# Low parts of the wide merge-gate weights formed by accumulating transfers from GpSimd

## The chip, the core and the metric

The kernel runs on one core of one Trainium2 chip. The core has a matrix engine (TensorE, PE in the profile, with its weight loads as PEld), a vector engine (VectorE, DVE), an activation engine (ScalarE, ACT), a general engine (GpSimd, POOL), a queue that issues transfers (SyncE, SP), and 16 DMA engines that carry out the transfers of all queues. The metric is the device time of one execution in microseconds (us), the median of several runs.

## What is computed

One layer of a hybrid decoder block on 512 tokens of width 2048, in float32. The part that matters here is the large input projection and the merge at the end:

```
u    = rmsnorm(x)                      # 512 x 2048
proj = u @ w_in                        # w_in: 2048 x 20528
...                                    # mLSTM branch -> h_a, gated DeltaNet branch -> h_b
gate_a, gate_b = last 2 x 2048 columns of proj
y    = sigmoid(gate_a) * (h_a @ w_out[:2048]) + sigmoid(gate_b) * (h_b @ w_out[2048:])
out  = rmsnorm(x + y)
```

The columns of `proj` from 16432 on are the pre-activations of the merge gates: 4096 columns, two per output channel.

## The kernel before

**Products in two parts.** Matrix products are made of operands of type float32r, which carry fewer bits than float32. To keep accuracy each operand is split into a high part (the value rounded to float32r) and a low part (what rounding left). A product is the sum of three: high x high, high x low, low x high. For the activations u the two parts are made once (`uh`, `ul`). For the weights they are made on the fly from each raw tile.

**The weight stream.** A list `plan` holds every weight part in the order of use: 768 parts, each 256 KB. A part is either two row blocks of 128 rows by 256 columns (kind "i"), one row block by 512 columns of `w_in` (kind "w"), or the same of `w_out` (kind "o"). Three steps are taken for each part, and each runs ahead of the products:

- `load_raw` (line 135) takes a buffer of the ring `wr` (4 buffers) and lets SP issue the transfer from memory (line 145).
- `split_next` (line 148) takes a buffer each of the rings `wh` and `wl` (4 buffers each). ACT copies the raw tile into the float32r high part (`split_hi`, line 112). DVE subtracts that from the raw tile and writes the low part (`split_lo`, line 115).
- `next_w` (line 157) hands the parts to the products. When part i is used, raw loads up to part i + 4 and splits up to part i + 3 have been written down.

A buffer is reused as soon as its last reader is done: a raw buffer after the two split instructions, a `wh`/`wl` buffer after the last matmul of the part.

**The order of work.** PE's instructions run in the order in which the program writes them. On the other engines a scheduler places the instructions by priority; the loads and splits are raised above the rest. Each engine then runs its queue in order: an instruction that waits holds up all behind it.

**The stages.** First the activations and the projections of the two branches run as twelve units, with the work of the branches filled in between. Then come the merge gates (the loop of line 880): four narrow blocks of 256 columns (`proj_tm`, kind "i", lines 226 to 229), and six wide blocks of 512 columns (`proj_wide`, kind "w", lines 241 to 243). A wide block has 16 parts; a part is used by 12 matmuls, three for each of the four groups of 128 tokens, in the order uh x high, uh x low, ul x high. At the end of a block ACT makes the tanh of four PSUM tiles (line 895) and SP stores them to memory (line 896). Last comes the output projection (kind "o", lines 935 to 937).

While the wide blocks run, the branch output `h_a` is loaded back for the output projection: `load_h` (line 862) loads 16 tiles `hr` through the same ring `wr` (line 867) and splits them on ACT and DVE into `hh` and `hl` with the same two functions. `load_x` (line 872) loads x again into `hf`.

GpSimd issues no transfer anywhere in this kernel. Kind "w" also occurs earlier, for the values of the mLSTM branch (columns 2048 to 4095).

Of the kernel before, what the change touches and what calls it, by code (L numbers as in the profile page):

```python
# [8 lines left out]
F32 = mybir.dt.float32  # L9
F32R = mybir.dt.float32r  # L10
AF = mybir.ActivationFunctionType
ALU = mybir.AluOpType
# [3 lines left out]
P = 128  # L16
# [6 lines left out]
NO = 512  # L23
# [14 lines left out]
GATE = 16432  # L38
# [9 lines left out]
def hybrid_block(  # L48
# [18 lines left out]
    V, A, G, T = nc.vector, nc.scalar, nc.gpsimd, nc.tensor  # L67
# [43 lines left out]
    def split_hi(hi, src):  # L111
        A.copy(hi, src)  # L112

    def split_lo(lo, src, hi):
        V.tensor_tensor(out=lo, in0=src, in1=hi.bitcast(F32), op=ALU.subtract)  # L115


    plan = []
# [13 lines left out]
    raws, parts = [], []  # L132
# [15 lines left out]
    def split_next():  # L148
        raw, nk, n = raws[len(parts)]
        with tc.high_priority(offset=2 * PRIO if len(parts) > SAHEAD else 0):  # L150
            hi = wp.tile([P, nk, n], F32R, tag="wh", name="wh", bufs=NSPL)
            lo = wp.tile([P, nk, n], F32R, tag="wl", name="wl", bufs=NSPL)
            split_hi(hi, raw)
            split_lo(lo, raw, hi)
        parts.append((hi, lo))

    def next_w(kind, c, k):
        i = used[0]
        assert plan[i] == (kind, c, k)
        used[0] += 1  # L160
        while len(raws) < min(len(plan), i + RAHEAD + 1):
            load_raw()
        while len(parts) < min(len(plan), i + SAHEAD + 1):
            split_next()
        return parts[i]
# [755 lines left out]
    for nb in range(D // NO):  # L921
        nsl = slice(nb * NO, (nb + 1) * NO)
        for br in range(2):
# [19 lines left out]
            for kt in range(KT - last):  # L943
                w = next_w("o", nb * NO, base + kt)
# [52 lines left out]
```

## Time and profile before

| What | Value |
|---|---|
| Median of 3 runs | 2379.36 us (2378.52 to 2379.41) |
| The profiled execution | 2379.44 us |
| Its span in the trace | 2377.7 us, granted clock 0.998 |
| Transfers over the whole span | 265.94 MB, mean 112 GB/s |
| Casts of a weight part to its high part (line 112) | 768, 475.7 us, 621 ns each |
| Subtractions for its low part (line 115) | 768, 550.1 us, 718 ns each |
| Matmuls of the wide gate blocks | 1152, 389 ns each, pipelined |
| Loads of a raw part issued by SP | 768 of 256 KB, 2.8 us (w_in) and 3.1 us (w_out) to landing, median |

The span is the time from the first to the last recorded instruction of one execution; some 1.7 us of the execution lie around it. Busy times of matmuls overlap, since the next one starts before the last has drained: the length of one (389 ns) is not the pace at which they start. A row of the timeline gives the start, the length, the engine, the line, the operation, the tile written and the tiles read, and in brackets how long the engine stood idle before it and what ended that.

### The profile page before, as it was taken

The numbers are of one execution on the slowest core, as the hardware profiler recorded it, in microseconds if no ns is written. First come the engines' busy times: TensorE is split into PE (matmuls) and PEld (weight loads), VectorE is DVE, ScalarE is ACT, GpSimd is POOL, SyncE is SP. The second block draws the span as 40 slices with busy tenths as digits, with TensorE's granted clock in tenths as the row PEclk, the third lists the DMA queues.
The fourth block names the chain that finished last, engine by engine and source line by source line (L and its number), as shares of the span: only waits on it lengthen the run. The fifth ranks groups of instructions, "written<-read, shape, count | busy, mean of one in ns | idle before, by whom it ended". The sixth has DMA issues, their size and how long they took to land. (4 is left out here: it accounts for less than half of the span.)

```text
span 2377.7 us, 32465 instructions
## 1 busy us (share of the span) xinstructions
PE 2344.2 (99%) x11999; PEld 1953.4 (82%) x11999; DVE 1145.5 (48%) x2307; ACT 826.5 (35%) x1854; POOL 237.0 (10%) x319
## 2 busy tenths in 40 slices
PE   6999999999999999999999999999999999999998
PEld 5888888888888888888888888888998888888886
DVE  5433767433485833348583324958333222434334
ACT  5323434332343423243343224433333323322222
POOL 0000212100021210011220002112000000010010
PEclk9999999999999999999999999999999999999999
DMA  5433334333333333333342333333375544634333
GB/s 147 114 96 102 94 100 100 94 98 98 98 94 98 107 89 98 97 94 98 96 120 74 107 97 92 96 93 103 91 233 147 159 115 122 207 114 128 121 115 129
DMA packets 232354, 265.94 MB, mean 112 GB/s; under 512 B 46337, under 2 KB 171490, under 8 KB 232194
## 3 DMA queue, kind: packets, MB, share of 16 engines
q1 hardware_dynamic: 232130, 263.79, 39.1%
q8 instruction: 94, 1.54, 0.3%
q14 instruction: 66, 0.54, 0.1%
q10 hardware_dynamic: 64, 0.07, 0.0%
HBM read 239.61 MB, written 24.18 MB: 111 GB/s over the span
## 5 line engine op out<-in xcount | busy, mean ns | idle before, releaser
L115 DVE TENSOR_TENSOR wl<-wr,wh 128x512 fp32r<-128x512 f32 x768 | 550.1, 718 | 875.3 <-ACT wh L112 850.3
L112 ACT CAST wh<-wr 128x512 fp32r<-128x512 f32 x768 | 475.7, 621 | 1148.5 <-PE pj L212 565.4
L211 PE MATMUL pj<-uh,wh 128*128 128x512 f32 x1792 | 736.4, 411 | 2.1 <-ACT yp L442 1.6
L213 PE MATMUL pj<-uh,wl 128*128 128x512 f32 x1792 | 701.4, 391 | 0.0
L212 PE MATMUL pj<-ul,wh 128*128 128x512 f32 x1792 | 699.9, 391 | 0.0
L213 PEld LDWEIGHTS pj<-uh,wl 128*128 128x128 f32 x1792 | 336.5, 188 | 74.5 <-DVE wl L115 0.4
L211 PEld LDWEIGHTS pj<-uh,wh 128*128 128x128 f32 x1792 | 337.4, 188 | 67.1 <-ACT yp L442 2.9
L212 PEld LDWEIGHTS pj<-ul,wh 128*128 128x128 f32 x1792 | 337.9, 189 | 60.5
L935 PE MATMUL py<-wh,hh 128*128 128x512 f32 x512 | 199.2, 389 | 0.0
L936 PE MATMUL py<-wl,hh 128*128 128x512 f32 x512 | 199.2, 389 | 0.0
L937 PE MATMUL py<-wh,hl 128*128 128x512 f32 x512 | 199.2, 389 | 0.0
L241 PE MATMUL pg<-wh,uh 128*128 128x512 f32 x384 | 149.4, 389 | 0.0
L242 PE MATMUL pg<-wl,uh 128*128 128x512 f32 x384 | 149.4, 389 | 0.0
L243 PE MATMUL pg<-wh,ul 128*128 128x512 f32 x384 | 149.4, 389 | 0.0
L936 PEld LDWEIGHTS py<-wl,hh 128*128 128x128 f32 x512 | 96.1, 188 | 20.1
L935 PEld LDWEIGHTS py<-wh,hh 128*128 128x128 f32 x512 | 96.1, 188 | 20.0
L937 PEld LDWEIGHTS py<-wh,hl 128*128 128x128 f32 x512 | 96.1, 188 | 19.8
L241 PE MATMUL pv<-wh,uh 128*128 128x512 f32 x256 | 99.6, 389 | 0.0
L242 PE MATMUL pv<-wl,uh 128*128 128x512 f32 x256 | 99.6, 389 | 0.0
L243 PE MATMUL pv<-wh,ul 128*128 128x512 f32 x256 | 99.6, 389 | 0.0
L530 DVE TENSOR_TENSOR tmp<-ls,xi 32x31 f32<-32x31 f32 (+15 forms) x248 | 91.1, 367 | 5.2 <-DMA ls<-ld 1.7
L532 DVE TENSOR_TENSOR xi<-xi,tmp 32x31 f32<-32x31 f32 (+15 forms) x248 | 87.0, 351 | 4.0
(249 smaller groups left out, 2457.8 us busy)
## 6 DMA issues: line engine op xcount, KB each, us to landing
wr<-in_w_in_dram SPq DMA_DIRECT2D x640, 256.0 KB, 2.8
wr<-in_w_out_dram SPq DMA_DIRECT2D x128, 256.0 KB, 3.1
hr<-h_d SPq DMA_DIRECT2D x32, 256.0 KB, 3.5
tgl<-tg_d SPq DMA_DIRECT2D x32, 256.0 KB, 3.3
tg_d<-tgw SPq DMA_DIRECT2D x24, 256.0 KB, 3.8
xt<-in_x_dram SPq DMA_DIRECT2D x8, 512.0 KB, 9.0
gb<-rows_d SPq DMA_DIRECT2D x16, 256.0 KB, 3.4
h_d<-mg SPq DMA_DIRECT2D x16, 256.0 KB, 3.1
```

Of the source, the lines that this page charges most:

```text
L112: A.copy(hi, src)
L115: V.tensor_tensor(out=lo, in0=src, in1=hi.bitcast(F32), op=ALU.subtract)
L211: T.matmul(ps[j], hi[:, k, wsl], uh[:, kt, :], start=(kt == 0), stop=False)
L212: T.matmul(ps[j], hi[:, k, wsl], ul[:, kt, :], start=False, stop=False)
L213: T.matmul(ps[j], lo[:, k, wsl], uh[:, kt, :], start=False, stop=(kt == KT - 1))
L241: T.matmul(ps[c], uh[:, kt, tsl], hi[:, 0, :], start=(kt == 0), stop=False)
L242: T.matmul(ps[c], uh[:, kt, tsl], lo[:, 0, :], start=False, stop=False)
L243: T.matmul(ps[c], ul[:, kt, tsl], hi[:, 0, :], start=False, stop=(kt == KT - 1))
L530: V.tensor_tensor(out=tv, in0=ls[:, i, i + 1:BS].unsqueeze(2).to_broadcast([NSYS, n, m]), in1=xi[:, i, 0:m].unsqueeze(1).to_broadcast([NSY ...
L935: T.matmul(ps[c], hh[base][:, kt, tsl], hi[:, 0, :], start=(kt == 0), stop=False)
L936: T.matmul(ps[c], hh[base][:, kt, tsl], lo[:, 0, :], start=False, stop=False)
L937: T.matmul(ps[c], hl[base][:, kt, tsl], hi[:, 0, :], start=False, stop=(kt == KT - 1))
```

## The change

For the wide merge-gate blocks, 96 of the 768 parts, the subtraction on DVE is replaced by two steps. ACT writes minus the high part into the low tile. Then GpSimd issues a transfer that reads the same 128 x 512 piece of `w_in` from memory once more and adds it onto the low tile in SBUF, so that the tile ends as raw minus high. The raw load by SP and the cast by ACT stay; all other parts are split as before.

```diff
             hi = wp.tile([P, nk, n], F32R, tag="wh", name="wh", bufs=NSPL)
             lo = wp.tile([P, nk, n], F32R, tag="wl", name="wl", bufs=NSPL)
             split_hi(hi, raw)
-            split_lo(lo, raw, hi)
+            kind, c, k = plan[len(parts)]
+            if kind == "w" and c >= GATE:
+
+                A.mul(lo, hi.bitcast(F32), -1.0)
+                G.dma_start(lo[:, 0, :], w_in[k * P:(k + 1) * P, c:c + NO], accum_op=ALU.add)
+            else:
+                split_lo(lo, raw, hi)
         parts.append((hi, lo))
```

## The prediction

> **What bounds the kernel now.** I read the busy shares first, then the stretch that the change touches, then the order of work inside it.
>
> ```profile
> PE 2344.2 (99%) x11999; PEld 1953.4 (82%) x11999; DVE 1145.5 (48%) x2307; ACT 826.5 (35%) x1854; POOL 237.0 (10%) x319
> 1756.70:2017.80 261.10, 261.10 (x1154) 216.20 (x1153) 75.56 (x111) 81.30 (x134) 0.00 (x0) 1.00 0.48 139
> ACT wh L112 <- PE pg L243: 155.9, 81, 2.1
> ACT hh L112 <- DMA hr<-h_d: 19.3, 12, 5.4
> ACT tgw L895 <- DMA tg_d<-tgw: 1.9, 4, 0.7
> ```
>
> The first line is the page: PE is busy for 99% of the span. The second is the table by stretches, for the six wide merge-gate blocks (first matmul into pg at 1756.7, last at 2017.6 us): its columns are length, sum, PE, PEld, DVE, ACT, POOL (busy and count), granted clock, DMA share and GB/s. PE is busy for all 261.1 us at clock 1.00, DVE for 75.56, POOL for none; DMA moves 139 GB/s at a share of 0.48. The last three lines are from the waits of that stretch. PE is in none of them: the split waits for PE, never PE for the split. So nothing can be gained here; PE time can be lost, if a low part arrives late.
>
> How much room there is comes from the timeline inside a quiet block:
>
> ```profile
> 1868.42 0.62 ACT L112 CAST wh<-wr 128x512 fp32r<-128x512 f32 x1 [2.10 <-PE pg L243]
> 1871.14 0.62 ACT L112 CAST wh<-wr 128x512 fp32r<-128x512 f32 x1 [2.10 <-PE pg L243]
> 1870.94 0.39 PE L241 MATMUL pg<-wh,uh 128*128 128x512 f32 x1
> 1871.80 0.69 DVE L115 TENSOR_TENSOR wl<-wr,wh 128x512 fp32r<-128x512 f32 x1 [2.03 <-ACT wh L112]
> ```
>
> Columns: start, length, instruction, idle before and its releaser. Casts come every 2.72 us: one weight part is 12 matmuls, so PE's pitch is 0.227 us. A cast starts when PE has finished the part four earlier, 0.20 us after the next part's first matmul (1870.94). That cast is for the part that starts three parts later, whose second matmul is the first to read the low part: 1870.94 + 3 x 2.72 + 0.23 = 1879.33. Today the low part is there at 1872.49, 6.84 us early. That is the whole cover.
>
> **What the change does, step by step.**
>
> Removed: 96 subtractions on DVE (6 blocks x 16 parts), 96 x 0.692 = 66 us of DVE. DVE is 29% busy here and nothing waits for it except SP, which reloads a raw buffer after the subtraction. Worth 0 on the path; raw buffers come free one subtraction (0.69 us) earlier, and the cast finds its raw part already landed, so that is 0 too.
>
> Added on ACT: 96 negations of 128x512. The nearest row is ACT's own ACTIVATE of 128x512 from SBUF to SBUF (the tanh of line 448, 632 ns); taken 0.63 us. ACT's groups hold a single table load in the whole kernel, although scaled copies (lines 284, 823) already alternate with tanh, so no reload is counted. ACT goes from 81 to 142 us of 261: not a bound. Cast, handover 0.04 and negation put the transfer's start at 0.62 + 0.04 + 0.63 + 0.04 = 1.33 us after the cast's start. What is left for issue plus landing is 1879.33 - 1871.14 - 1.33 = 6.86 us.
>
> Added on POOL: 96 issues. POOL has nothing else between 1716 and about 2080 us, so nothing is queued behind them but the next issue. The trace has no transfer issued by POOL. Bounds: below, SP's issue of the same tile, 0.33 us; above, POOL's own full 128x512 operation (line 959), 1.58 us. I take 1.0, the row of a tiny POOL operation in this stretch (line 676, 1008 ns), as a fixed price of a POOL instruction. All are under 2.72, so POOL sets no rate.
>
> Added on the DMA engines: 96 transfers that read 256 KB of weights and also read and rewrite 256 KB of lo.
>
> ```profile
> wr<-in_w_in_dram SPq DMA_DIRECT2D x640, 256.0 KB, 2.8
> xt<-in_x_dram SPq DMA_DIRECT2D x8, 512.0 KB, 9.0
> hr<-h_d SPq DMA_DIRECT2D x32, 256.0 KB, 3.5
> hf<-in_x_dram SPq DMA_DIRECT2D x8, 512.0 KB, 6.1
> ```
>
> These are the issue rows; the last number is the time to landing. No accumulating transfer is among them. Bounds: 2.8 us if it lands like the raw load of the same tile, 9.0 like the 512 KB loads of x at the start. Since two reads of 256 KB feed it while raw loads run beside it, I take the 512 KB row of this part of the kernel, 6.1.
>
> Issue plus landing is then A = 7.1 us (bounds 3.1 and 10.6), against a cover of 6.86. When A exceeds it, three parts take 1.30 + A (0.20 + 1.33 - 0.23 = 1.30), so the pitch of a part is (1.30 + A)/3 = 2.80 instead of 2.72, and 96 x 0.08 = **7.7 us**.
>
> **Entry into the stretch.** Here the cover is smaller:
>
> ```profile
> 1754.88 0.62 ACT L112 CAST hh<-hr 128x512 fp32r<-128x512 f32 x1 [6.02 <-DMA hr<-h_d]
> 1755.40 1.14 ACT L112 CAST wh<-wr 128x512 fp32r<-128x512 f32 x2
> 1763.47 0.62 ACT L112 CAST hh<-hr 128x512 fp32r<-128x512 f32 x1 [5.42 <-DMA hr<-h_d]
> ```
>
> ACT's queue stands 6.02 us behind a cast that waits for an hr load, and the cast of wide part 1 comes only at 1755.40. Its low part would be in at 1755.40 + 1.33 + 7.1 = 1763.8; its first use is due at 1756.9 + 2.72 = 1759.6. PE stops **4.2 us** (nothing for A up to 2.9).
>
> **Block ends.** At five ends inside the stretch ACT also runs four tanh of 0.6 us; in the 2.72 us around 1798 it would now start six instructions where it starts them 0.54 apart (1.14 us for two casts), 3.2 us: a cast or negation about 1.0 us late (estimate), 5 x 1.0 = **5 us**.
>
> **The hr casts.** 12 casts of hh wait for their load (19.3 us in all) and stand ahead of a weight cast. If the hr load lands 2.6 us later beside the accumulates (6.1 for 3.5), less the 0.69 us by which its buffer is free earlier, ACT is 1.9 us later, and the next weight cast has 0.89 us of idle before it (1784.10): 1.0 us late each. I count half of the twelve, **6 us**, because the first ones coincide with the entry stall.
>
> Sum: 7.7 + 4.2 + 5 + 6 = 23 us. The profiled execution took 2379.44 us (span 2377.7 and 1.7 around it); the median of the three runs is 2379.36, the same within 0.1. Forecast **2402 us**. At the lower bounds of issue and landing (A = 3.1) the cost is 0.2 us of entry stall. At the upper ones the pitch is 3.97, so 120 us, and the entry 7.7: 2507.
>
> **Rivals.**
>
> *Hidden after all (not slower).* The place is the 6.86 us cover. If issue plus landing stays under about 6.0 us, steady pitch and block ends cost nothing and only the entry stall of at most 3.1 us and some hr casts remain: 2380 to 2384. For it: the raw loads of the same size land in 2.8 us, and from 1900 to 2020 the DMA share is only 0.41 to 0.42. Against: an hr load took 7.8 us just before the stretch (issued 1747.10, ACT released 1754.88). The Trainium skill, "DMA: Bandwidth & Descriptors", section "Anatomy of one DMA", gives 2.0 us plus bytes over 436 GB/s for a transfer issued by GpSimd; for 256 KB that is an estimate of 2.6 us and this rival's time.
>
> *The DMA engines become the bound.* The stretch now moves 261.1 x 139 GB/s = 36.3 MB. The accumulates add 96 x 0.262 x 2 = 50.3 MB if both reads count: 86.6 MB. At the present cost of a byte (0.48 share for 36.3 MB) that is a share of 1.15, 299 us, +38; at the 251 GB/s of the busiest 30 us just before (1720 to 1750), 345 us, +84. So 2417 to 2463. Against: that window showed a share of 0.79 and was not full; if only one read counts, the share is 0.81 and all fits. The Trainium skill, "Collectives: The Full Stack", section "The bandwidth ceiling: the fold count and why AG ≠ RS ≠ AR", says that an add inside the DMA costs no time by itself but needs two source reads, which halved the rate there (62.28 against 32.35 GB/s). By it both reads count and this rival's 2417 to 2463 stand; no run shown here has such a transfer.
>
> *Issue or landing far off the rows.* An issue over 2.72 us makes POOL the bound: 4 us would be 96 x 1.28 = 123 us, 2502, and every further us 96 more. The rows neither show nor exclude this.
>
> *Faster.* Only if PE gained; it has no wait and the full clock in the stretch. That the accumulate does not do what it says I see no way for: a low part is read only after its transfer's completion.
>
> **Numbers.** Forecast case (landing-limited, 2385 to 2412) 0.43; hidden 0.27; DMA-bound 0.15; far off the rows 0.12; faster 0.03. Taking 0.2% (4.8 us) as what a measurement of this kernel can tell from no change: faster 0.03, same 0.27, slower 0.70. Range 2378.5 to 2507: it leaves out most of "faster" and the upper part of the last rival.
>
> **What would show it.** In the changed profile: PE idle within 1756 to about 2040 us, put down to the landing of wl; a pitch of casts above 2.72 us; POOL issues near 1 us; landing of wl near 6 us; the longest PE wait near the first wide parts. POOL issues back to back with no idle would mean the third rival; a DMA share near 1.0 the second; PE at 261 us without waits the first. A landing under 5 us, or hr loads no later than now, would make the forecast wrong.

## The result and the profile after

The changed kernel takes 2410.99 us (median of 4 runs, 2404.23 to 2413.61) against 2379.31 us before (4 runs, 2378.52 to 2379.41): 31.7 us slower, ratio 1.0129 with a 95% interval of 1.0117 to 1.0142. The runs of the changed kernel spread over 9.4 us, those of the kernel before over 0.9. The profiled execution is one of the longer ones, 2413.15 us with a span of 2411.4. Line numbers are 6 higher than before from the edit on: the wide products are now lines 247 to 249, the tanh is line 901, the negation line 157, GpSimd's issue line 158.

From the page of the changed kernel (busy shares; the wide products that read a low part, with busy time, mean ns, idle time of PE before them and what ended it; transfer queues with packets, MB and share of the 16 DMA engines; issue rows with microseconds to landing at the end):

```profile
PE 2352.2 (98%) x11999; PEld 1954.4 (81%) x11999; DVE 1078.9 (45%) x2211; ACT 882.2 (37%) x1950; POOL 319.7 (13%) x415
...
L248 PE MATMUL pg<-wl,uh 128*128 128x512 f32 x384 | 152.7, 398 | 24.9 <-DMA wl<-in_w_in_dram 24.9
...
q1 hardware_dynamic: 232130, 263.79, 37.1%
q0 software_dynamic: 13824, 25.17, 6.6%
...
wr<-in_w_in_dram SPq DMA_DIRECT2D x640, 256.0 KB, 2.8
...
wl<-in_w_in_dram POOLq DMA_DIRECT2D x96, 256.0 KB, 5.5
hr<-h_d SPq DMA_DIRECT2D x32, 256.0 KB, 3.9
```

The 96 new transfers are queue q0. They land 5.5 us after their issue began (4.1 to 9.5), twice as late as the raw load of a tile of the same size. That median mixes two halves: 6.6 us for those issued between 1790 and 1890 us, 4.7 us from 1900 us on. Their share gives a price: 6.6% of 2411.4 us is 159 us of each DMA engine, 1.66 us for a transfer. The same sum for q1 (37.1%, 1006 times 256 KB) gives 0.89 us for 256 KB moved plainly, as an average over all the transfers of that queue.

The table by stretches of the changed kernel (length, sum, PE, PEld, DVE, ACT, POOL, granted clock, DMA share, GB/s):

```profile
1756.70:1790.00 33.30, 27.34 (x110) 21.71 (x108) 2.08 (x3) 14.43 (x25) 9.57 (x11) 0.90 0.88 214
1790.00:1900.00 110.00, 95.80 (x403) 75.56 (x402) 6.92 (x10) 50.36 (x86) 28.87 (x33) 0.98 0.90 207
1900.00:2051.00 151.00, 146.29 (x643) 120.26 (x642) 2.08 (x3) 72.18 (x119) 44.65 (x51) 1.00 0.96 210
```

The six wide blocks now last from 1756.5 to 2050.8 us, 294 where they lasted 261. PE is idle for 6.0, 14.2 and 4.7 us of the three stretches, 24.9 in all, and PE's list of waits has that very number for 17 waits on the landing of `wl`. The rest of the 33 us is not idle: the clock column falls to 0.90 and 0.98.

What one of the 17 waits looks like, in rows picked from the timeline of the changed kernel:

```profile
1790.19 0.62 ACT L112 CAST wh<-wr 128x512 fp32r<-128x512 f32 x1 [1.43 <-PE pg L249]
1793.38 0.62 ACT L112 CAST hh<-hr 128x512 fp32r<-128x512 f32 x1 [2.57 <-DMA hr<-h_d]
1793.90 0.63 ACT L157 ACTIVATE wl<-wh 128x512 fp32r<-128x512 f32 x1
1794.83 0.88 POOL L158 DMA_DIRECT2D wl<-in_w_in_dram  x1 [4.90 <-ACT wl L157]
1800.78 0.47 PE L248 MATMUL pg<-wl,uh 128*128 128x512 f32 x1 [0.80 <-DMA wl<-in_w_in_dram]
```

The cast of the weight part is on time. Behind it in ACT's queue, ahead of the negation, stands a cast of `hh` that waits 2.57 us for its load. The negation comes 3.1 us later than it could, the transfer takes 6 us, and PE stands for 0.80 us. This comes back every 9 to 10 us for the most part, with each hr load.

### The profile page after: what moved, and what is told of

Read it like the earlier page. It is cut to its first block, busy times and chain, and to the rows that moved or that the text cites. A ratio compares the mean times of both kernels' runs of the same rounds, so it can differ in the third digit from the quotient of the medians.

```text
span 2411.4 us, 32751 instructions
## 1 busy us (share of the span) xinstructions
PE 2352.2 (98%) x11999; PEld 1954.4 (81%) x11999; DVE 1078.9 (45%) x2211; ACT 882.2 (37%) x1950; POOL 319.7 (13%) x415
## 3 DMA queue, kind: packets, MB, share of 16 engines
q1 hardware_dynamic: 232130, 263.79, 37.1%
## 5 line engine op out<-in xcount | busy, mean ns | idle before, releaser
L115 DVE TENSOR_TENSOR wl<-wr,wh 128x512 fp32r<-128x512 f32 x672 | 482.9, 720 | 871.7 <-ACT wh L112 844.4
L248 PE MATMUL pg<-wl,uh 128*128 128x512 f32 x384 | 152.7, 398 | 24.9 <-DMA wl<-in_w_in_dram 24.9
L158 POOL DMA_DIRECT2D wl<-in_w_in_dram x96 | 84.2, 877 | 242.2 <-ACT wl L157 218.3
L248 PEld LDWEIGHTS pg<-wl,uh 128*128 128x128 f32 x384 | 73.0, 190 | 46.5 <-issue 8.8
```

Of the source, the lines that this page charges most:

```text
L158: G.dma_start(lo[:, 0, :], w_in[k * P:(k + 1) * P, c:c + NO], accum_op=ALU.add)
L248: T.matmul(ps[c], uh[:, kt, tsl], lo[:, 0, :], start=False, stop=False)
```

## Experiments

Two theories stood against each other. **A**: the transfers fit, but ACT's queue doesn't: the negation stands behind casts of `hh` that wait for hr loads. **B**: the 16 DMA engines are full and set the time by bytes. All times are medians; the kernel before took 2379.4 to 2379.8 us beside them. In the code shown, a remark behind `#` names the run and is not part of the code.

### Where in the stretch, and whether ACT alone

`e2_late_blocks`, the last three of the six wide blocks only; `e8_early_blocks`, the first three only:

```diff
-            if kind == "w" and c >= GATE:
+            if kind == "w" and c >= GATE + 5 * NO:           # e2
+            if kind == "w" and GATE <= c < GATE + 5 * NO:    # e8
```

> Only the last three of the six wide blocks use the accumulating transfers; no hr load runs beside them, and there the changed profile has a DMA share of 0.98 to 0.99. Theory A: only the few stalls of that half stay, 2382 to 2388 us. Theory B: the fullest half of the stretch keeps its cost, half of 32 us or more, 2393 to 2400 us.

> Only the first three wide blocks, with the hr loads beside them, use the accumulating transfers. Theory A: nearly the whole cost, 2402 to 2410 us. Theory B: the lesser half of the cost, 2389 to 2396 us.

Measured: 2384.31 us for the late half (ratio 1.0019, 1.0009 to 1.0028) and 2406.66 for the early half (1.0113, 1.0098 to 1.0128). That is 4.7 and 27.1 us over the kernel before, together 31.8, the whole of the 31.7. Nearly all of the cost lies in the half where hr loads run beside the accumulates; the entry into the stretch, with the loads of x and of the final weights, is in that half too. Both are as A said; B in this form, with the cost spread by the fullness of the engines, falls.

`e3_negate_add`, the negation without the transfer:

```diff
-                G.dma_start(lo[:, 0, :], w_in[k * P:(k + 1) * P, c:c + NO], accum_op=ALU.add)
+                V.tensor_tensor(out=lo, in0=raw, in1=lo.bitcast(F32), op=ALU.add)
```

> ACT writes minus the high part as in the change, but DVE adds the raw tile onto it in place of the transfer. Theories A and B: without the transfer nothing is late, 2379 to 2382 us. Rival C (the 96 added ACT instructions of 0.63 us are what is too much): 2390 us or more.

Measured: 2379.08 us (0.9998, 0.9988 to 1.0007). The 96 added ACT instructions cost nothing; C falls.

### ACT's queue taken away

`e1_hh_on_dve` moves the casts of the first 16 hh tiles to DVE. `e5_negate_first` forms minus the high part from the raw tile ahead of the cast. `e6_both` does both.

```diff
-            split_hi(hh[base][:, k, :], raw)                 # e1, e6
+            if base:
+                split_hi(hh[base][:, k, :], raw)
+            else:
+                V.tensor_copy(hh[base][:, k, :], raw)
...
-            split_hi(hi, raw)                                # e5, e6
...
-                A.mul(lo, hi.bitcast(F32), -1.0)
+                A.mul(lo, raw, -1.0)
                 G.dma_start(lo[:, 0, :], w_in[k * P:(k + 1) * P, c:c + NO], accum_op=ALU.add)
+                split_hi(hi, raw)
             else:
+                split_hi(hi, raw)
```

> The casts of the 16 hh tiles that are loaded beside the gate blocks move from ACT to DVE, which is idle there; the accumulating transfers stay. Theory A (a low part comes late because ACT's cast and negation stand in queue behind an hh cast that waits for its hr load): most of the 32 us go, 2383 to 2393 us. Theory B (the 16 DMA engines, at a share of 0.86 to 0.99 in the changed profile, set the time by the bytes they move): the bytes are the same, so 2404 to 2414 us as with the change.

> ACT forms minus the high part straight from the raw tile, ahead of the cast, so the transfer can be issued 0.66 us earlier and no other instruction stands between cast and negation; work and bytes are the same. Theory A: each late landing is later by 0.6 to 3 us less, 2390 to 2402 us. Theory B: no change, 2404 to 2414 us.

> The hh casts on DVE and the negation ahead of the cast together. Theory A: nothing of the loss but single late landings, 2379 to 2386 us. Theory B: 2404 to 2414 us.

Measured: 2402.94 (1.0096, 1.0081 to 1.0111), 2404.81 (1.0104, 1.0087 to 1.0121) and 2401.34 us (1.0094, 1.0079 to 1.0109). So 8.0, 6.2 and 9.6 us come back; for e5 that is not clear of the spread, since its interval overlaps that of the change (1.0117 to 1.0142). e6, with no hh cast in ACT's queue before 2040 us and 0.66 us more cover, is outside A's range and 3 us below B's; 22 us stay. A alone falls as well. Where the rest sits is in the stretches of e1, with the same early stretch of the changed kernel after it:

```profile
1756.70:1900.00 143.30, 132.65 (x576) 106.78 (x575) 14.79 (x27) 63.76 (x105) 41.51 (x48) 1.00 0.98 227
```

```profile
1756.70:1900.00 143.30, 123.14 (x511) 97.27 (x510) 9.00 (x13) 64.80 (x111) 38.44 (x44) 0.96 0.89 208
```

With ACT's queue out of the way the engines go from a share of 0.89 to 0.98 in the early half. And in e6 a new wait has come up, from ACT's waits of that kernel (us in total, times, longest):

```profile
ACT wl L156 <- DMA wr<-in_w_in_dram: 30.8, 13, 4.6
```

The raw loads themselves are now late; before the change ACT had no wait on them between 1756 and 2018 us. So I formed **B2**: the engines are full only where hr loads run beside the accumulates. From the queue shares, one part needs 0.89 (raw load) + 1.66 (accumulate) + 0.30 (a third of an hr load) + 0.22 (a quarter of a 256 KB store) = 3.07 us of each engine in the early half, against 2.72 us of matmuls; 48 parts of that are 17 us over. In the late half it is 2.77, at the edge. These are estimates from the shares.

### What a transfer costs

`e4_plain_copy` leaves out the add: the low part is the raw tile.

```diff
-                G.dma_start(lo[:, 0, :], w_in[k * P:(k + 1) * P, c:c + NO], accum_op=ALU.add)
+                G.dma_start(lo[:, 0, :], w_in[k * P:(k + 1) * P, c:c + NO])
```

> GpSimd's transfer writes the weights into the low tile and doesn't add, so the low part is the raw tile and the output isn't the reference's; the negation by ACT and the issue stay. What differs is the read of the destination and the add. Theory A: if the landing falls from 5.5 to about 3 to 4 us, the transfer is inside its cover of 6.9 us more often and 2385 to 2400 us remain, with PE's waits where ACT is behind an hh cast. Theory B: the stretch moves 25 MB less, the DMA share falls to about 0.7 and with it the whole loss, 2379 to 2383 us. If the landing stays near 5.5 us, the add costs nothing by itself and the time stays at 2404 to 2414 us.

Measured: 2391.52 us (1.0051, 1.0036 to 1.0066). Landing falls from 5.5 to 3.6 us in the median, POOL's issue from 877 to 541 ns, and the engine time:

```profile
q0 software_dynamic: 13824, 25.17, 4.0%
```

4.0% of 2389.1 us over 96 is 1.00 us, so an accumulating transfer costs an engine about 1.7 times a plain one from the same queue. Of the 31.7 us 12 stay; inside A's range, and 8 us above B's. By the sum of B2 a part now needs 0.89 + 1.00 + 0.30 + 0.22 = 2.41 us of each engine, less than the 2.72 of the matmuls, so B2 alone doesn't explain these 12 us either.

`e7_from_sbuf` adds from the raw tile in SBUF instead of from memory:

```diff
-                G.dma_start(lo[:, 0, :], w_in[k * P:(k + 1) * P, c:c + NO], accum_op=ALU.add)
+                G.dma_start(lo[:, 0, :], raw[:, 0, :], accum_op=ALU.add)
```

> The accumulating transfer takes its addend from the raw tile in SBUF and not from memory; it moves as many bytes, but holds the raw buffer until it has landed, some 6 to 7 us longer, so the next raw load of the ring of four starts that much later. Theory A: landing near 5 us, and the later raw loads add new waits of the cast: 2405 to 2450 us. Theory B: as many bytes for the engines, 2404 to 2414 us. If reading memory is what makes the landing long, landing falls under 4 us.

Measured: 2410.47 us (1.0128, 1.0111 to 1.0145), as with the change. Landing is 1.0 us shorter (4.5, not under 4) and a transfer takes an engine 1.51 us; the raw buffer is held until it lands, and ACT now waits 43.1 us for raw loads between 1756 and 2055 us, where it had no such wait with the change. The two theories share this time, so it does not tell them apart.

### Load against queue

`f1_alternate`: every second part; `f2_half_width`: all parts, half the columns; `f3_half_width_hh_dve`: as f2, with the hh casts on DVE as in e1. `f4_unused_stores` is the kernel before with two stores per wide part that nobody needs.

```diff
-            if kind == "w" and c >= GATE:                                            # f1
+            if kind == "w" and c >= GATE and k % 2 == 0:
...
-                G.dma_start(lo[:, 0, :], w_in[k * P:(k + 1) * P, c:c + NO], accum_op=ALU.add)  # f2, f3
+                G.dma_start(lo[:, 0, 0:NB], w_in[k * P:(k + 1) * P, c:c + NB], accum_op=ALU.add)
...
             split_lo(lo, raw, hi)                                                    # f4, on the kernel before
+            kind, c, k = plan[len(parts)]
+            if kind == "w" and c >= GATE:
+                j = len(parts) - plan.index(("w", GATE + GNARROW * NB, 0))
+                G.dma_start(scr_d[2 * j], hi.bitcast(F32)[:, 0, :])
+                G.dma_start(scr_d[2 * j + 1], lo.bitcast(F32)[:, 0, :])
```

> Every second part of all six wide blocks uses the accumulating transfer, 48 as in the kernels with three blocks. By the queue shares an accumulating transfer takes each DMA engine 1.66 us, a plain 256 KB load 0.89. Theory B2 (the engines are full where hr loads run beside the accumulates, 0.89 + 1.66 + 0.30 + 0.22 = 3.07 us per part against 2.72 us of matmuls): 2.24 us per part with every second one, so room, 2380 to 2386 us. Theory A (ACT's queue behind the hh casts decides): half of the cost stays, 2391 to 2398 us.

> The transfer adds onto the first 256 columns of each low tile only; the other half of the low part is minus the high part, so the output isn't the reference's. ACT's work and queue are those of the change; the engines' time per part falls by half of 1.66 us, to 2.24. Theory B2: the loss is gone but for the entry, 2380 to 2388 us. Theory A: ACT stands behind the hh casts as before, only the landing is about 1 us shorter, 2392 to 2404 us.

> As the run before (half of the low part not completed), and the hh casts beside the gate blocks on DVE. With the queue and the load both gone, theories A and B2 say 2379 to 2384 us; more would mean that a third cause is open.

> The kernel before, with two plain 256 KB stores per wide part from GpSimd into an unused buffer in memory, of the high and the low part; nobody waits for them but the reuse of the buffers. The engines get about 2 x 0.89 = 1.78 us more per part, as much as from the accumulates. Theory B2: raw and hr loads come late and 10 us or more are lost, 2390 to 2405 us. Theory A: no low part waits for a transfer, 2379 to 2384 us.

Measured: f1 2386.81 (1.0032, 1.0021 to 1.0043), f2 2388.97 (1.0040, 1.0025 to 1.0055), f3 2382.72 (1.0012, 1.0003 to 1.0021), f4 2395.99 us (1.0076, 1.0059 to 1.0093). f1 and f2 lie 1 us above the ranges of B2 and 3 to 4 below those of A; f3 is inside the common range; f4 is inside B2's and 12 us above A's. The relief in f1 and f2 was smaller than expected: a transfer of half the width took an engine 0.97 us (3.9% of 2386.6 us over 96), not half of 1.66, and one of f1 1.79 us (3.6% of 2383.0 us over 48).

f4 is the cleanest of them: no low part depends on a transfer, the splits are those of the kernel before, and 16.2 us are lost to load. The stores also hold the `wh` and `wl` buffers until they have landed, but only two waits, of DVE and 2.3 us together, are put down to that. Its stretch shows where the time goes, in ACT's waits and PE's longest:

```profile
ACT hh L113 <- DMA hr<-h_d: 83.9, 15, 8.0
ACT wh L113 <- DMA wr<-in_w_in_dram: 10.7, 8, 3.1
PE pg L247 <- ACT wh L113: 6.3, 3, 3.6
```

(In the kernel before, the first of these was 29.9 us between 1756 and 2040.) The hr loads land late, and the weight casts stand behind them. From 1900 to 2020 us, with no hr loads, PE has no idle at a DMA share of 0.92. In f4 an engine carries about 1.3 us more per part (5.4% of 2391.4 us over 96), a little less than with the change.

f1 and e8 have the same 48 accumulates: spread thinly they cost 7.1 us, in three blocks beside the hr loads 27.1. f2 and f3 differ only in the place of the hh casts: 9.2 against 3.0.

The change, e1, f2 and f3 make a table of two by two. Over the kernel before they cost, with the hh casts on ACT, 31.7 us at full width and 9.2 at half width; with these casts on DVE, 23.4 and 3.0. So moving the casts is worth 6 to 8 us, and halving the transfer 20 to 23, whichever is done first. What halving takes away is time on the engines and landing together (3.5 us instead of 5.5).

## Why the prediction came out right, and where its terms did not

The measured time, 2411.0 us, lies 9 us above the forecast of 2402, inside the range and just inside the forecast case's span (2385 to 2412). The kind of loss is the one forecast: PE stands in the wide blocks, put down to the landing of `wl`, longest near the first parts. Point by point:

**What was removed.** Worth nothing, as said; the 96 negations are free, too (e3).

**Issue and landing.** Taken as 1.0 + 6.1 = 7.1 us; measured 0.88 us to issue and, from the start of the issue to landing, 6.6 us in the median between 1790 and 1890 and 4.7 from 1900 us on. The cover was taken as 6.86 us with 0.04 from negation to issue; that step took 0.29 (the negation of 1891.35 ends at 1891.98, the issue starts at 1892.27), which leaves 6.6. So the landing just reaches the cover and doesn't exceed it, and the *steady pitch* term, 7.7 us, was not there: without an hr load POOL's issues come 2.72 us apart (1892.27, 1894.99, 1897.71), the pace of the matmuls. This is the first error of the sum: a cover that is used up costs nothing by itself, but what is left of it, nothing beside the hr loads and some 2 us after them, is too little for the delays that the old 6.84 us swallowed.

**Entry.** Forecast 4.2 us of standing; measured 1.45 + 4.51 = 6.0. Wide part 1 was behind the same hh cast as before (1754.76), and beside the loads of x and of the final weights the first two transfers landed after 8.6 and 8.9 us, where 7.1 was taken. Then PE ran at half pace for a while, which the sum did not have:

```profile
1765.88 0.77 PE L248 MATMUL pg<-wl,uh 128*128 128x512 f32 x1 [4.51 <-DMA wl<-in_w_in_dram]
1766.44 0.63 PE L249 MATMUL pg<-wh,ul 128*128 128x512 f32 x1
1766.87 0.63 PE L247 MATMUL pg<-wh,uh 128*128 128x512 f32 x1
...
1771.21 0.39 PE L249 MATMUL pg<-wh,ul 128*128 128x512 f32 x1
1771.44 0.39 PE L247 MATMUL pg<-wh,uh 128*128 128x512 f32 x1
```

Starts are 0.43 us apart until 1770.7 and 0.23 after.

**Block ends.** Forecast 5 us for five ends, from ACT having too many instructions. The late half has three waits, all at a block's end: 1.86, 2.02 and 0.82 us, 4.7 in all, and e2 costs 4.7 us. The size is near for another reason than the one given:

```profile
1913.64 1.56 ACT L901 ACTIVATE tgw<-pg 128x512 f32<-128x512 f32 x3
1915.17 0.62 ACT L112 CAST wh<-wr 128x512 fp32r<-128x512 f32 x1
1915.83 0.63 ACT L157 ACTIVATE wl<-wh 128x512 fp32r<-128x512 f32 x1
1918.82 0.60 ACT L901 ACTIVATE tgw<-pg 128x512 f32<-128x512 f32 x1 [2.36 <-DMA tg_d<-tgw]
1919.31 0.61 ACT L112 CAST wh<-wr 128x512 fp32r<-128x512 f32 x1
```

The fourth tanh waits 2.36 us for a buffer whose store has not landed, and the next cast stands behind it. In the kernel before the four such waits were at most 0.7 us; the stores of the tanh tiles now land in 4.8 us instead of 3.8.

**The hr casts.** This is the mis-sized term. The mechanism was named (a later hr load holds ACT, and a weight cast behind it), and 1.0 us was worked out for each of twelve; then only half were counted, 6 us, because the first ones were to coincide with the entry stall. The loads themselves landed as late as was feared: 6.2 us in the median between 1757 and 1900 us (6.1 forecast), where it was 3.0 before. Measured between 1790 and 1885: twelve waits of PE, 14.2 us; ten follow an `hh` cast that stood for its load, two (0.18 and 0.37 us) come right after the tanh of a block's end. ACT's waits from 1790 to 1900 in the changed kernel, and those from 1784 to 1862 in the kernel before:

```profile
ACT hh L112 <- DMA hr<-h_d: 31.8, 10, 4.5
```

```profile
ACT hh L112 <- DMA hr<-h_d: 7.8, 8, 2.3
```

3.2 us each against 1.0, so 2.2 later where 1.9 was forecast. The ground for halving did not hold: two of the changed kernel's twelve such waits of ACT lie before 1790 us, and with no cover left nearly every later one goes on to PE.

**Not in the sum.** Two restarts at half pace (18 matmuls, 0.2 us each, 3.6 us), and 0.2 to 0.3 us beyond the recorded idle at each of the 17 waits, since the matmuls then don't overlap: some 4 us.

The sum came near because a term that did not exist (7.7) nearly made up for restarts that were left out; that is luck. What it then fell short by is mostly the hr term, 14.2 us for 6. Of the causes, the experiments bear out the delayed hr loads and casts; a landing longer than the cover in the steady state, which gives the forecast case its name, did not happen in the median.

**The rivals.** Hidden: no; PE waits 17 times. But it nearly holds for the late half, where 48 transfers cost 4.7 us. The DMA engines as the bound: weighted at 0.15, it holds a large part of the loss. Its sum (share 1.15 for both reads) was near, since a share of 0.93 over a stretch that became 13% longer is 1.05 of the old length; its time, 2417 us and more, was not reached. It was set out as another case than the forecast; f4 shows load alone losing 16 us through the very queues that the forecast named, and f3 shows that with the load halved and the hh casts moved 3 us are left. The load makes hr, raw and store landings late, ACT's in-order queue hands that to the weight parts, and the accumulate's own landing has used up the cover that would have swallowed it. How the 22 to 23 us left in e1 and e6 divide between late raw loads and the accumulate's landing was not separated. POOL as the bound: no, 0.88 us of 2.72.

On the rule about two reads: the Trainium skill, "Collectives: The Full Stack", section "The bandwidth ceiling: the fold count and why AG ≠ RS ≠ AR", has a factor of 1.93 between its rates without and with the add; here the engine time went from 1.00 to 1.66 us, a factor of about 1.7. The 2.6 us estimated with the Trainium skill, "DMA: Bandwidth & Descriptors", section "Anatomy of one DMA — SWDGE (gpsimd) path", is below what was measured beside other traffic: medians of 3.6 us for the plain transfer (3.1 at the least) and 5.5 for the accumulating one.

## What to carry to other kernels

Work taken from an engine that nothing waits for gained nothing here, and giving it to the DMA engines spends something that every load shares: price a new transfer by its time on the engines (here 1.66 us, against 0.89 for a plain 256 KB) and add it to what runs beside it, stage by stage, before looking at its own latency. When a step uses up the lookahead of a ring, small waits that were harmless (a cast behind another tile's load, a tanh behind a store) all reach the bound engine. Placing the same 48 transfers away from the hr loads and the entry made the difference between 27 and 5 us.

## What the runs showed of the hardware

PE's pace after a wait: 0.43 us from start to start, instead of 0.23, after recorded waits of 4.51 us (until 4.8 us later, granted clock 0.50) and of 2.70 us (until 3.1 us later) in the changed kernel. In e2 a wait of 1.88 us was enough, and the pace was halved from the first matmul behind it. In e7 it fell 1.1 us after a wait of 3.05, in e8 at 1817.3 us, 1.5 us after one of only 1.82. A wait of 2.87 us in e1 was followed by the full pace. So the length of one wait alone doesn't decide. The Trainium skill, "TensorE: Matmul & The Clock Gate", section "Part 1: The HAM clock gate", describes a gate that halves the clock after an idle window of some 3.4 us on a free-running count; the halving agrees (granted clock 0.50), but here recorded waits of 2.70 and 1.88 us were enough.

An accumulating transfer of 256 KB from GpSimd takes POOL 0.88 us to issue, where the plain one takes 0.54, and lands 1.9 us later. Taking its addend from SBUF instead of memory shortens the landing by 1.0 us.
